# One-hots built as outer products of two small tables, and another order of VectorE's work at the end of the spread, in a two-layer encoder with product-key experts

## The chip, the cores and the metric

The kernel runs on one core of one Trainium2 chip. The metric is device time in microseconds (us), smaller is better. A core has TensorE (PE; its weight loads are shown apart, as PEld), VectorE (DVE), ScalarE (ACT), GpSimd (POOL) and SyncE (SP, which issues the DMAs here). Each works through its own queue in order, and waits on semaphores for the others.

## What is computed

Two layers over 256 tokens of width 1024: layer 0 is differential attention and an expert mixer (PEER), layer 1 is stick-breaking attention and another expert mixer. Each sub-layer is followed by a normalisation. Only the expert mixer matters for the change:

```
q = (x @ w_pq)                                  # 8 heads, two halves of 64
scores = q . sub_keys                           # 128 keys per half
s_top, i_top = top_k(scores, 16)                # per half
cand = s_top[0][:, None] + s_top[1][None, :]
g_s, g_i = top_k(cand, 16)                      # 16 of 256 candidates per head
id = i_top[0] * 128 + i_top[1]                  # one of 16384 experts
gate = softmax(g_s)
h = gelu(x . u[id]);   out = sum(gate * h * v[id])
```

A token chooses 8 heads x 16 = 128 experts. An expert's number is a row I (0 to 127) times 128 plus a column J (0 to 127).

## The kernel before

The kernel does the expert mixer without gathering. It computes gelu(x . u) for all 16384 experts as 128 units of 128 experts (a unit is one row I: all its columns J on the partitions, 256 tokens along the free axis), forms the matrix of gates in the same layout, multiplies both (the "weighing"), and multiplies by all of v. A product of two f32 numbers on TensorE is done in three passes, with each f32 operand split in a high part h (rounded by ScalarE, line 151) and a low part l = raw - h (VectorE or GpSimd, line 156). A unit of u or v is 512 KB: one DMA into `raw`, one h, one l. The rings of `raw`, `h` and `l` have 3 tiles each, so a DMA waits until the split of three units earlier has read its tile.

The stages of one expert mixer, in each of the two layers:

- **Routing** (`routing`, lines 669 to 781): scores, two top-16 searches, the arithmetic that turns the place among the candidates into I and J (`ef`), softmax of the gates (`gx`). Three transposes (lines 774 to 776) bring I, J and the gate to the layout "chosen expert on the partitions, token on the free axis", and ScalarE and VectorE put them into `idxT` as f16: row 0 is I, row 1 is J, rows 2 and 3 are the gate's high and low part. This is done once for each half b of the tokens. While it runs, TensorE computes the first 42 units of u ("stored" in `big`).
- **Spread** (lines 863 to 883): 32 iterations of 8 tokens. For a token, the 128x128 matrix of gates is the product of two one-hot matrices, summed over the 128 chosen experts: `oa` (I equals the column) and `gh`, `oj` (J equals the column, times the gate's high or low part). VectorE makes the four 1024-element f16 products of an iteration (lines 867, 868, 869, 872), TensorE does 16 small matmuls (878, 879) into two PSUM tiles, and `drain` of the next iteration takes them out: rows below 42 by VectorE, with the weighing (859), the others by ScalarE (860). Between the one-hot matmuls TensorE does 18 matmuls of the next units of u in each iteration (`next(ex)`, line 802); a unit has 24, so 3 iterations of 4 begin one, and with it `Hidden.pair` calls `fetch`, whose l is placed behind that iteration's one-hots in VectorE's order. The order of TensorE and VectorE is written out by hand here (`manual_schedule`). The five tiles of tag `oh` are shared by the three names.
- **Weighing and the product with v** (lines 911 to 957): for s = 0 to 64 the loop takes pair `order[s - 1]` of units, splits two units of v and does 24 passes (line 207). `prep(order[s])` makes wh and wl of the next pair's weighted activations (921, 922), and calls `weigh(2)`, which multiplies two more pairs by their gates (909). VectorE's order is by hand until s = 6, then the scheduler's.

At the end of the spread VectorE's order by hand is: last `drain`, `weigh(2)`, wl of pair 0, `weigh(2)`, l of unit 67 of u, l of unit 68, wl of pair 1, `weigh(2)`, l of the first two units of v, and so on. The l of unit 67 stands there since `pair` fetches a unit when it begins the one before.

Of the kernel before, what the change touches and what calls it, by code (L numbers as in the profile page):

```python
# [10 lines left out]
F32 = mybir.dt.float32  # L11
# [9 lines left out]
P = 128  # L21
# [6 lines left out]
HP = 8  # L28
# [30 lines left out]
def trunk(ctx: ExitStack, tc: tile.TileContext, x, xT, ln_g, ln_b, w_qkv, w_o_a, lam_p, subln, w_kv,  # L59
# [30 lines left out]
    nc.vector.tensor_scalar(ntri, jp, 0.0, -1.0, OP.is_le, OP.mult)  # L90
    nones = const.tile([P, P], F32, name="nones")
    nc.vector.memset(nones, -1.0)
    cmask = const.tile([P, P], BF16, name="cmask")
# [7 lines left out]
    nc.vector.tensor_copy(iota2, iota.unsqueeze(2).to_broadcast([P, P, 2]))  # L101
    off16 = const.tile([P, K, K], F16, name="off16")
    len16 = const.tile([P, K, K], F16, name="len16")
    for a, off, n in SPANS:
        nc.gpsimd.memset(off16[:, a, :], float(off))
        nc.gpsimd.memset(len16[:, a, :], float(SPANS[a - 1][2]) if a else 0.0)
    row16 = const.tile([P, K, K], F16, name="row16")
    nc.vector.tensor_copy(row16, iota[:, 0:K].unsqueeze(2).to_broadcast([P, K, K]))
    mhalf = const.tile([P, 8], F32, name="mhalf")
# [535 lines left out]
    def peer(layer, xh, xl, spill, o_res):  # L645
# [6 lines left out]
        for n in range(4):  # L652
            nc.scalar.activation(qp[:, 2 * n:2 * n + 2, :], aq[n], AF.Copy)
        idxT = work.tile([P, 4, T], F16, name="idxT", bufs=1)
        hx = {}

        def scores(b):
# [11 lines left out]
        def routing(b, sc):  # L669
# [16 lines left out]
            sm = reg(o + 1560, 2, HP)  # L686
            ef = reg(o + 1576, 2, HP, K)
            cc = half(o + 1832, HP, K)
            stp = half(o + 1896, HP, K, K)
            prd = half(o + 2920, HP, K, K)  # L690
            s16l = s16.rearrange("p h c k -> p (h c) k")
# [72 lines left out]
            yield 3.8  # L764
            ef = ef.rearrange("p c h k -> p (c h k)")
            gx = s16.rearrange("p h c k -> p (h c k)")[:, 0:P].rearrange("p (h k) -> p h k", k=K)
# [5 lines left out]
            yield 2.0  # L772
            pt = psum.tile([P, 3, P], F32, name="acc", tag="acc")
            nc.tensor.transpose(pt[:, 0, :], ef[:, 0:P], ident)
            nc.tensor.transpose(pt[:, 1, :], ef[:, P:2 * P], ident)
            nc.tensor.transpose(pt[:, 2, :], gx.rearrange("p h k -> p (h k)"), ident)
            bs = slice(b * P, (b + 1) * P)
            nc.scalar.activation(idxT[:, 0:2, bs], pt[:, 0:2, :], AF.Copy)
            nc.scalar.activation(idxT[:, 2, bs], pt[:, 2, :], AF.Copy, scale=GS)
            nc.vector.scalar_tensor_tensor(idxT[:, 3, bs], pt[:, 2, :], GS, idxT[:, 2, bs], OP.mult, OP.subtract)  # L780
            yield 0.5

        class Hidden:
# [77 lines left out]

        i2 = iota2.unsqueeze(1).to_broadcast([P, 4, P, 2])
        for t8 in range(0, T, 8):
            col = [idxT[:, c, t8:t8 + 8].rearrange("p (r t) -> p r t", t=2).unsqueeze(2).to_broadcast([P, 4, P, 2])
                   for c in range(4)]
            oj, gh, oa = (work.tile([P, 4, P, 2], F16, name=m, tag="oh", bufs=OH) for m in ("oj", "gh", "oa"))
# [48 lines left out]
        def prep(i):  # L915
# [7 lines left out]
            wq[i] = (wh, wl)  # L923
            weigh(2)

# [120 lines left out]
```

## Time and profile before

| | us |
|---|---|
| median of 3 runs | 1948.08 (1941.38 to 1950.44) |
| profiled execution, its own time | 1947.43 |
| its span, first to last instruction | 1945.7 |
| PE busy | 1861.1 (96%) |
| DVE busy | 1259.7 (65%) |
| ACT busy | 913.1 (47%) |
| POOL busy | 209.1 (11%) |

The span is what the trace covers; the profiled execution took 1.7 us more than that. A busy share is an average over stages: TensorE's 96% says where the work is, not what a single stage waits for.

### The profile page before, as it was taken

To read this page: it belongs to the slowest core of one execution; us is meant where nothing else is said; L and a number is where in the kernel's file an instruction comes from. 1 tells how busy PE (TensorE), PEld (TensorE's weight loads), DVE (VectorE), ACT (ScalarE), POOL (GpSimd) and SP (SyncE) were. 2 spreads that over 40 slices of the span, in tenths; PEclk is the share of its full clock that TensorE was granted. 3 is DMA by queue.
4 is the path that set the end of the run, shared out by engine and by line. 5 is a ranking of instruction groups with operands and counts; after the bars stand their busy time and mean duration, and the time that the engine had idled before them with its cause. 6 is when DMAs were issued, how large, how long until landed. Compare 5 with 4: busy or idle time off the path is not lost.

```text
span 1945.7 us, 30827 instructions
## 1 busy us (share of the span) xinstructions
PE 1861.1 (96%) x12244; PEld 1669.0 (86%) x12244; DVE 1259.7 (65%) x2300; ACT 913.1 (47%) x1244; POOL 209.1 (11%) x144
## 2 busy tenths in 40 slices
PE   8999999889999999999999899998899999999997
PEld 7779998887899999988798699988878999999886
DVE  5467988996455555565552479889865555555655
ACT  4444445444444444454446454454444444444543
POOL 5425400000000000000142253000000000000001
PEclk9888999999999999999999999999999999999999
DMA  6433544225555555565633235433355555555753
GB/s 218 170 119 119 179 147 152 99 98 179 189 192 189 193 179 190 191 240 192 211 128 133 109 131 184 151 132 109 107 186 176 194 183 186 195 183 184 249 194 131
DMA packets 90449, 325.40 MB, mean 167 GB/s; under 512 B 10176, under 2 KB 10560, under 8 KB 89664
## 3 DMA queue, kind: packets, MB, share of 16 engines
q1 hardware_dynamic: 90304, 323.43, 48.9%
q8 instruction: 96, 1.57, 0.3%
q14 instruction: 49, 0.40, 0.1%
HBM read 320.24 MB, written 3.15 MB: 166 GB/s over the span
## 4 chain that ended last, share of the span: by engine, by line
PE 77%; DVE 18%; issue 2%; DMA 1%; ACT 1%; POOL 0%; SPq 0%; ACTq 0%; DVEq 0%; POOLq 0%
PE acc L207 40%; PE w L802 26%; DVE l L156 3%; PE acc L252 2%; DVE gh L869 2%; DVE oj L872 2%; DVE oj L867 1%; PE acc L446 1%; DVE big L859 1%; PE w L252 1%; DVE big L330 1%; PE w L207 1%; PE w L468 1%; DVE big L699 1%; DVE big L701 1%
## 5 line engine op out<-in xcount | busy, mean ns | idle before, releaser
L151 ACT ACTIVATE h<-raw 128x1024 fp32r<-128x1024 f32 x579 | 607.0, 1058 | 850.4 <-PE acc L207 474.6
L156 DVE TENSOR_TENSOR l<-raw,h 128x1024 fp32r<-128x1024 f32 x526 | 642.9, 1234 | 537.4 <-ACT h L151 537.4
L802 PE MATMUL w<-xh,l 128*128 128x256 f32 x2048 | 580.4, 285 | 11.6 <-DVE l L156 10.9
L802 PE MATMUL w<-xh,h 128*128 128x256 f32 x2048 | 586.1, 286 | 1.8 <-ACT h L151 1.8
L802 PE MATMUL w<-xl,h 128*128 128x256 f32 x2048 | 580.4, 284 | 0.0
L802 PEld LDWEIGHTS w<-xh,l 128*128 128x128 f32 x2048 | 392.6, 192 | 18.5 <-DVE l L156 12.6
L207 PE MATMUL acc<-l,wh 128*128 128x512 f32 x1024 | 401.2, 393 | 7.4 <-DVE l L156 7.4
L207 PE MATMUL acc<-h,wl 128*128 128x512 f32 x1024 | 401.3, 393 | 0.0
L802 PEld LDWEIGHTS w<-xh,h 128*128 128x128 f32 x2048 | 393.9, 192 | 7.5 <-ACT h L151 2.3
L802 PEld LDWEIGHTS w<-xl,h 128*128 128x128 f32 x2048 | 393.7, 192 | 4.7
L207 PE MATMUL acc<-h,wh 128*128 128x512 f32 x1024 | 279.7, 392 | 1.6 <-ACT h L151 1.6
L207 PEld LDWEIGHTS acc<-l,wh 128*128 128x128 f32 x1024 | 193.7, 189 | 44.4 <-DVE l L156 7.8
L207 PEld LDWEIGHTS acc<-h,wl 128*128 128x128 f32 x1024 | 194.0, 189 | 37.2
L207 PEld LDWEIGHTS acc<-h,wh 128*128 128x128 f32 x1024 | 189.3, 189 | 38.0 <-ACT h L151 2.0
L156 POOL TENSOR_TENSOR l<-raw,h 128x1024 fp32r<-128x1024 f32 x53 | 127.8, 2415 | 174.3 <-ACT h L151 171.6
L180 POOL TENSOR_TENSOR ahead<-big,ahead 128x512 fp32r<-128x512 f32 x18 | 24.1, 1369 | 765.8 <-ACT ahead L170 765.8
L922 DVE TENSOR_TENSOR wl<-big,wh 128x512 fp32r<-128x512 f32 x128 | 86.9, 687 | 16.6 <-ACT wh L921 10.1
L879 PE MATMUL acc<-oa,oj 128*128 128x128 f16 x512 | 66.1, 220 | 28.8 <-DVE oj L872 28.8
L303 POOL TENSOR_TENSOR mv<-mv,mhalf 128x1 f32<-128x1 f32 x8 | 4.9, 607 | 762.9 <-DVE mv L302 762.9
L921 ACT ACTIVATE wh<-big 128x512 fp32r<-128x512 f32 x128 | 78.1, 619 | 13.0 <-DVE big L909 8.7
L879 PEld LDWEIGHTS <-oj 128*128 128x128 f16 x512 | 48.6, 97 | 35.1 <-DVE oj L872 35.0
L860 ACT ACTIVATE big<-acc 128x344 f32<-128x344 f32 x128 | 51.5, 453 | 49.3 <-DVE big L859 49.2
(210 smaller groups left out, 1855.7 us busy)
## 6 DMA issues: line engine op xcount, KB each, us to landing
raw<-in_uT SPq DMA_DIRECT2D x256, 512.0 KB, 3.4
raw<-in_v SPq DMA_DIRECT2D x256, 512.0 KB, 3.3
raw<-in_w_qkv SPq DMA_DIRECT2D x23, 512.0 KB, 4.0
raw<-in_w_kv SPq DMA_DIRECT2D x12, 512.0 KB, 4.0
raw<-in_w_o_a SPq DMA_DIRECT2D x8, 512.0 KB, 3.9
big<-in_w_pq SPq DMA_DIRECT2D x8, 512.0 KB, 6.7
raw<-in_w_pq SPq DMA_DIRECT2D x8, 512.0 KB, 5.6
raw<-in_w_q SPq DMA_DIRECT2D x8, 512.0 KB, 4.3
```

The lines of the kernel that those rows point to most:

```text
L151: self.h = nc.scalar.activation(h, raw, AF.Copy)
L156: o = e.tensor_tensor(l, raw, h.bitcast(F32), OP.subtract)
L180: o = nc.gpsimd.tensor_tensor(l[f], self.raws[d][:, f * 512:(f + 1) * 512], h[f].bitcast(F32), OP.subtract)
L207: nc.tensor.matmul(acc[b][f], a[:, d, ts], w[:, fs], start=(first and q == 0), stop=(last and q == 2))
L252: nc.tensor.matmul(acc[n // 2][:, n % 2, :], w[:, c:c + P], a[:, d, :], start=(d == 0 and q == 0 and n % 2 == 0), stop=(d == DC - 1 and q ...
L802: nc.tensor.matmul(ps[:, k, :], w[:, ds], a[:, d, :], start=(d == 0 and q == 0), stop=(d == DC - 1 and q == 2))
L860: nc.scalar.activation(wv[:, N_STORED:], pv[:, N_STORED:], AF.Copy, scale=1.0 / GS)
L869: nc.vector.tensor_tensor(gh, oj, col[2], OP.mult)
L872: nc.vector.tensor_tensor(oj, oj, col[3], OP.mult)
L879: nc.tensor.matmul(ps[:, k, :], oj[:, m, :, e], oa[:, m, :, e], start=False, stop=True)
L921: nc.scalar.activation(wh, s, AF.Copy)
L922: nc.vector.tensor_tensor(wl, s, wh.bitcast(F32), OP.subtract)
```

## The change

Each f16 column number J is written as 16 * (J >> 4) + (J & 15). A table of 8 columns says which J >> 4 a chosen expert has, one of 16 columns which J & 15, and a one-hot over 128 columns is the outer product of both. The gate is multiplied into the small table.

- Routing gains four VectorE instructions for each half of the tokens (a cast to integers, a shift, a mask, a cast back), a fourth transpose, and a fifth row of `idxT`.
- In the spread, `parts` runs once for 16 tokens (every second iteration) and makes `hi1` (which J >> 4, 128 elements), `lo` (256), `hi2` = hi1 times the gate's high part and `hi3` = hi1 times its low part (128 each). An iteration then has three large products in place of four: `oa`, `gh` = hi2 x lo, `oj` = hi3 x lo.
- `fetch` is called once more before the last `drain`, so that unit 67 is split ahead of it; `pair` then fetches only when fewer than two units are in hand.
- `weigh(2)` moves out of `prep`, and both stand behind the two splits of v in each step of the last loop.
- The tables `off16`, `len16` and `row16` of the routing move from a place of their own, filled once at the start, into `big`, filled by 48 memsets of GpSimd in each expert mixer. `nones` becomes a column read with step 0.

```diff
+        off16, len16, row16 = (
+            big[:, 17408 + i * 128:17408 + (i + 1) * 128].bitcast(F16).rearrange("p (a b) -> p a b", b=K) for i in range(3))
+        for a, off, n in SPANS:
+            nc.gpsimd.memset(off16[:, a, :], float(off))
+            nc.gpsimd.memset(len16[:, a, :], float(SPANS[a - 1][2]) if a else 0.0)
+            nc.gpsimd.memset(row16[:, a, :], float(a))
...
+            ei = i16.rearrange("p h c k -> p (h c k)").bitcast(I32).rearrange("p (c n) -> p c n", c=2)
+            nc.vector.tensor_copy(ei[:, 1], ef[:, 1])
+            nc.vector.tensor_scalar(ei[:, 0], ei[:, 1], 4, None, OP.logical_shift_right)
+            nc.vector.tensor_scalar(ei[:, 1], ei[:, 1], 15, None, OP.bitwise_and)
+            nc.vector.tensor_copy(ef[:, 1:3], ei)
...
-            pt = psum.tile([P, 3, P], F32, name="acc", tag="acc")
+            pt = psum.tile([P, 4, P], F32, name="acc", tag="acc")
...
             def pair(self, i, dst):
...
-                    self.fetch()
+                    if len(self.got) < 2:
+                        self.fetch()
...
+        NR = 8
+        hi1, hi2, hi3 = (work.tile([P, NR, 8, 2], F16, name=n, bufs=1) for n in ("hi1", "hi2", "hi3"))
+        lo = work.tile([P, NR, 16, 2], F16, name="lo", bufs=1)
+        def parts(t0):
...
+            nc.vector.tensor_tensor(hi1, i2[:, :, 0:8], col(1, 8), OP.is_equal)
+            nc.vector.tensor_tensor(lo, i2[:, :, 0:16], col(2, 16), OP.is_equal)
+            nc.vector.tensor_tensor(hi2, hi1, col(3, 8), OP.mult)
+            nc.vector.tensor_tensor(hi3, hi1, col(4, 8), OP.mult)
         for t8 in range(0, T, 8):
...
-            nc.vector.tensor_tensor(oj, i2, col[1], OP.is_equal)
-            nc.vector.tensor_tensor(oa, i2, col[0], OP.is_equal)
-            nc.vector.tensor_tensor(gh, oj, col[2], OP.mult)
+            if t8 % (2 * NR) == 0:
+                parts(t8)
+            rs = slice(t8 // 2 % NR, t8 // 2 % NR + 4)
+            def outer(dst, hi):
+                nc.vector.tensor_tensor(dst.rearrange("p r (a b) t -> p r a b t", b=16),
+                                        hi[:, rs].unsqueeze(3).to_broadcast([P, 4, 8, 16, 2]),
+                                        lo[:, rs].unsqueeze(2).to_broadcast([P, 4, 8, 16, 2]), OP.mult)
+            nc.vector.tensor_tensor(oa, i2, colI, OP.is_equal)
+            outer(gh, hi2)
             drain()
             prev = []
-            nc.vector.tensor_tensor(oj, oj, col[3], OP.mult)
+            outer(oj, hi3)
...
+        hidden.fetch()
         drain()
         ctx2.close()
...
         def prep(i):
...
             wq[i] = (wh, wl)
-            weigh(2)
...
-            if 0 < s < n:
-                prep(order[s])
-            if s == len(ext) // 2:
-                order_v.close()
             if s >= 1:
...
                             passes(acc, b, f, *args)
+                weigh(2)
+                if s < n:
+                    prep(order[s])
+            if s == len(ext) // 2:
+                order_v.close()
```

## Rows read from the trace of the kernel before

**Rows 1.** The page, busy us of each engine (share of the span) xinstructions.

```profile
PE 1861.1 (96%) x12244; PEld 1669.0 (86%) x12244; DVE 1259.7 (65%) x2300; ACT 913.1 (47%) x1244; POOL 209.1 (11%) x144
```

**Rows 2.** Windows by stage: us, busy us PE, PEld, DVE, ACT, POOL, PE clock, DMA.

```profile
314.00:426.00 112.00, 97.34 (x1015) 92.80 (x1014) 112.00 (x203) 51.99 (x94) 0.00 (x0) 1.00 0.32 109
...
504.00:830.00 326.00, 326.00 (x2089) 297.08 (x2088) 173.34 (x173) 148.24 (x174) 0.00 (x0) 1.00 0.56 188
```

**Rows 3.** Timeline of DVE in the spread of layer 0: start us, us, instruction.

```profile
334.51 0.68 DVE L872 TENSOR_TENSOR oj<-oj,idxT 128x1024 f16<-128x1024 f16 x1
335.11 1.22 DVE L156 TENSOR_TENSOR l<-raw,h 128x1024 fp32r<-128x1024 f32 x1
336.24 0.68 DVE L867 TENSOR_TENSOR oj<-iota,idxT 128x1024 f16<-128x1024 f16 x1
...
338.05 0.56 DVE L859 SCALAR_TENSOR_TENSOR big<-acc,big 128x168 f32<-128x168 f32 x2
338.53 0.68 DVE L872 TENSOR_TENSOR oj<-oj,idxT 128x1024 f16<-128x1024 f16 x1
```

**Rows 4.** Groups by form: shapes xcount | busy us, mean ns | idle before.

```profile
L867 DVE TENSOR_TENSOR oj<-iota,idxT 128x1024 f16<-128x1024 f16 x64 | 43.7, 682 | 4.1 <-ACT idxT L778 4.1
...
L752 DVE TENSOR_TENSOR big<-big,off 128x2048 f16<-128x2048 f16 x4 | 4.9, 1222 | 0.1
...
L740 DVE TENSOR_TENSOR big<-big 128x256 f16<-128x256 f16 x12 | 3.5, 292 | 0.4
...
L106 POOL MEMSET len<- 128x16 f16 x16 | 1.5, 115 | 0.0
```

**Rows 5.** Timeline of POOL before the first split of u, layer 0.

```profile
172.87 2.40 POOL L156 TENSOR_TENSOR l<-raw,h 128x1024 fp32r<-128x1024 f32 x1 [12.40 <-ACT h L151]
```

**Rows 6.** Timeline of DVE at the end of the routing, layer 0, second half.

```profile
300.99 0.28 DVE L769 TENSOR_REDUCE big<-big 128x8 f32<-128x128 f32 x1 [1.55 <-ACT big L768]
```

**Rows 7.** Timeline of DVE at the end of the spread, layer 0.

```profile
431.68 0.79 DVE L859 SCALAR_TENSOR_TENSOR big<-acc,big 128x168 f32<-128x168 f32 x2 [2.73 <-PE acc L879]
...
434.39 0.69 DVE L922 TENSOR_TENSOR wl<-big,wh 128x512 fp32r<-128x512 f32 x1
...
436.20 2.35 DVE L156 TENSOR_TENSOR l<-raw,h 128x1024 fp32r<-128x1024 f32 x2
444.08 0.69 DVE L922 TENSOR_TENSOR wl<-big,wh 128x512 fp32r<-128x512 f32 x1 [5.52 <-ACT wh L921]
...
445.89 2.35 DVE L156 TENSOR_TENSOR l<-raw,h 128x1024 fp32r<-128x1024 f32 x2
```

**Rows 8.** Timeline of ACT there: the split of v's second unit.

```profile
441.99 1.06 ACT L151 ACTIVATE h<-raw 128x1024 fp32r<-128x1024 f32 x1 [6.20 <-DMA raw<-in_v]
```

**Rows 9.** Timeline of PE there, with its waits; the last row is layer 1.

```profile
435.36 1.19 PE L207 MATMUL acc<-h,wh 128*128 128x512 f32 x4 [0.81 <-ACT h L151]
437.47 0.39 PE L802 MATMUL w<-xh,l 128*128 128x256 f32 x1 [0.93 <-DVE l L156]
...
447.16 0.80 PE L207 MATMUL acc<-l,wh 128*128 128x512 f32 x1 [4.15 <-DVE l L156]
...
1415.25 0.50 PE L207 MATMUL acc<-l,wh 128*128 128x512 f32 x1 [3.23 <-DVE l L156]
```

**Rows 10.** The chain that ended last: start us, us, what.

```profile
437.48 4.40 DMA raw<-in_v
447.16 56.66 PE acc L207 x236
...
521.13 2.75 PE acc L207 x12
...
1415.25 55.39 PE acc L207 x236
```

**Rows 11.** Window after that stall, columns as in rows 2.

```profile
446.00:450.00 4.00, 2.84 (x7) 2.29 (x8) 4.00 (x6) 0.55 (x2) 0.00 (x0) 0.55 0.43 139
```

More of the change, by code (lines that the diff above doesn't have):

```diff
@@ L90, in trunk @@
     nc.vector.tensor_scalar(ntri, jp, 0.0, -1.0, OP.is_le, OP.mult)
-    nones = const.tile([P, P], F32, name="nones")
-    nc.vector.memset(nones, -1.0)
+    none1 = const.tile([P, 1], F32, name="none1")
+    nc.vector.memset(none1, -1.0)
+    nones = none1.to_broadcast([P, P])
     cmask = const.tile([P, P], BF16, name="cmask")
@@ L653, in peer @@
             nc.scalar.activation(qp[:, 2 * n:2 * n + 2, :], aq[n], AF.Copy)
-        idxT = work.tile([P, 4, T], F16, name="idxT", bufs=1)
+        idxT = work.tile([P, 5, T], F16, name="idxT", bufs=1)
         hx = {}
+        off16, len16, row16 = (
[4 more added lines that the diff above has]
+            nc.gpsimd.memset(row16[:, a, :], float(a))
         def scores(b):
@@ L686, in routing @@
             sm = reg(o + 1560, 2, HP)
[L687 to L690, printed above, removed]
+            ef = reg(o + 1576, 3, HP, K)
+            cc = half(o + 1960, HP, K)
+            stp = half(o + 2024, HP, K, K)
+            prd = half(o + 3048, HP, K, K)
             s16l = s16.rearrange("p h c k -> p (h c) k")
@@ L772, in routing @@
             yield 2.0
-            pt = psum.tile([P, 3, P], F32, name="acc", tag="acc")
-            nc.tensor.transpose(pt[:, 0, :], ef[:, 0:P], ident)
-            nc.tensor.transpose(pt[:, 1, :], ef[:, P:2 * P], ident)
-            nc.tensor.transpose(pt[:, 2, :], gx.rearrange("p h k -> p (h k)"), ident)
+            pt = psum.tile([P, 4, P], F32, name="acc", tag="acc")
+            for c in range(3):
+                nc.tensor.transpose(pt[:, c, :], ef[:, c, :], ident)
+            nc.tensor.transpose(pt[:, 3, :], gx.rearrange("p h k -> p (h k)"), ident)
             bs = slice(b * P, (b + 1) * P)
-            nc.scalar.activation(idxT[:, 0:2, bs], pt[:, 0:2, :], AF.Copy)
-            nc.scalar.activation(idxT[:, 2, bs], pt[:, 2, :], AF.Copy, scale=GS)
-            nc.vector.scalar_tensor_tensor(idxT[:, 3, bs], pt[:, 2, :], GS, idxT[:, 2, bs], OP.mult, OP.subtract)
+            nc.scalar.activation(idxT[:, 0:3, bs], pt[:, 0:3, :], AF.Copy)
+            nc.scalar.activation(idxT[:, 3, bs], pt[:, 3, :], AF.Copy, scale=GS)
+            nc.vector.scalar_tensor_tensor(idxT[:, 4, bs], pt[:, 3, :], GS, idxT[:, 3, bs], OP.mult, OP.subtract)
             yield 0.5
@@ L862, in peer, with col @@
         i2 = iota2.unsqueeze(1).to_broadcast([P, 4, P, 2])
-        for t8 in range(0, T, 8):
-            col = [idxT[:, c, t8:t8 + 8].rearrange("p (r t) -> p r t", t=2).unsqueeze(2).to_broadcast([P, 4, P, 2])
-                   for c in range(4)]
-            oj, gh, oa = (work.tile([P, 4, P, 2], F16, name=m, tag="oh", bufs=OH) for m in ("oj", "gh", "oa"))
-            nc.vector.tensor_tensor(oj, i2, col[1], OP.is_equal)
-            nc.vector.tensor_tensor(oa, i2, col[0], OP.is_equal)
-            nc.vector.tensor_tensor(gh, oj, col[2], OP.mult)
+        NR = 8
+        hi1, hi2, hi3 = (work.tile([P, NR, 8, 2], F16, name=n, bufs=1) for n in ("hi1", "hi2", "hi3"))
+        lo = work.tile([P, NR, 16, 2], F16, name="lo", bufs=1)
+        def parts(t0):
+            def col(c, n):
+                a = idxT[:, c, t0:t0 + 2 * NR].rearrange("p (r t) -> p r t", t=2)
+                return a.unsqueeze(2).to_broadcast([P, NR, n, 2])
+            i2 = iota2.unsqueeze(1).to_broadcast([P, NR, P, 2])
+            nc.vector.tensor_tensor(hi1, i2[:, :, 0:8], col(1, 8), OP.is_equal)
+            nc.vector.tensor_tensor(lo, i2[:, :, 0:16], col(2, 16), OP.is_equal)
+            nc.vector.tensor_tensor(hi2, hi1, col(3, 8), OP.mult)
+            nc.vector.tensor_tensor(hi3, hi1, col(4, 8), OP.mult)
+        for t8 in range(0, T, 8):
+            if t8 % (2 * NR) == 0:
+                parts(t8)
+            rs = slice(t8 // 2 % NR, t8 // 2 % NR + 4)
+            colI = idxT[:, 0, t8:t8 + 8].rearrange("p (r t) -> p r t", t=2).unsqueeze(2).to_broadcast([P, 4, P, 2])
+            oj, gh, oa = (work.tile([P, 4, P, 2], F16, name=m, tag="oh", bufs=OH) for m in ("gl", "gh", "oa"))
+            def outer(dst, hi):
[4 more added lines that the diff above has]
+            outer(gh, hi2)
             drain()
             prev = []
-            nc.vector.tensor_tensor(oj, oj, col[3], OP.mult)
+            outer(oj, hi3)
             for r in range(2):
```

9 lines of the change are left out of this document (1 added, 8 removed).

## The prediction

> **What bounds the kernel now.** I read the page first. TensorE is busy for 96% of the span [rows 1], so for the kernel to get faster, TensorE has to wait less, or another engine has to stop holding it back; less work on VectorE, at 65%, is worth something only in a stage where TensorE waits for it. So I looked at windows by stage next. While u and v are both streamed (504 to 830 us) TensorE is busy for all of 326 us. In the spread of layer 0 it is busy for 97.34 of 112 us, and VectorE for all 112 [rows 2]: here VectorE is the limit. Layer 1 repeats this.
>
> The timeline of VectorE says what an iteration of the spread costs. A one-hot product lasts 0.68 us, but the next one starts 0.60 us after it: from 336.24, three of them bring us to the drain at 338.05. The two drains take 0.48, an l of u 1.13. From L872 at 334.51 to L872 at 338.53, one iteration with an l is 4.02 us [rows 3]; the iteration in four that begins no unit lacks the 1.13, so it is 2.89. Four iterations: 3 x 4.02 + 2.89 = 14.95 us, or 30 iterations in the 112 us window.
>
> Last, the end of the spread, where TensorE's timeline shows three waits in layer 0: 0.81, 0.93 and 4.15 us, together 5.89. In layer 1 the last of them is 3.23, the first two are the same: 4.97 [rows 9]. Here is how they come about. The last drain waits 2.73 us for the one-hot matmuls. Then VectorE does its list in order: wl of pair 0 at 434.39, and the l of units 67 and 68 only at 436.20 [rows 7]. TensorE waits for the first of these (the 0.93). The l of 67 also frees the raw tile for v's second unit: its DMA starts at 437.48 and takes 4.40 [rows 10], ScalarE waits 6.20 for it [rows 8], and wh of pair 1 is queued behind that split. VectorE waits 5.52 for this wh, and behind VectorE's wl stands the l of v's first unit, whose data were there long before; it comes at 445.89 [rows 7], and TensorE gets it at 447.16. One late split has put a DMA's latency on the path.
>
> The stall costs more than its idle time. After it the granted clock is 0.55 over four microseconds [rows 11], near the lower of the two levels (1.2 of 2.4 GHz), and the next 236 passes take 56.66 us in layer 0 and 55.39 in layer 1. At the later rate, 12 in 2.75 us, they are 54.08 [rows 10]: 2.6 and 1.3 us lost to the clock. So there is 5.89 + 2.6 = 8.5 us to be had in layer 0, and 4.97 + 1.3 = 6.3 in layer 1.
>
> **The change, part by part.**
>
> *The spread.* Each iteration loses one product of 1024 elements, 0.60 us; four iterations lose 2.41. `parts` is new, twice in four iterations: three instructions of 128 elements and one of 256, all f16. No row shows such small ones back to back, so I bound them. Two elements per cycle make 1024 elements 533 ns, and the 0.60 between starts leaves 0.07 for the instruction itself. By that, 128 elements are 0.136 and 256 are 0.20: 0.61 for one `parts`. From above: each lasts its full duration before the next starts. 256 elements f16 last 292 ns, 1024 last 682 [rows 4], so 128 last about 0.23, and the four 0.98, with gaps at most 1.1. I take 0.61: only hi2 depends closely on an earlier one, and `lo` stands between. Four iterations then are 14.95 - 2.41 + 2 x 0.61 = 13.76 us.
>
> Does the limit pass to TensorE? Its busy time of 97.34 us in 30 iterations [rows 2] is 13.0 for four, an upper bound since waiting at the start of a burst is counted in it. VectorE stays the limit, with less than a microsecond to spare; so a faster VectorE still would not bring much more. The saving is 1.19 us in four iterations, over 30 iterations of each layer: 7.5 x 1.19 x 2 = 17.9 us. With `parts` at 1.1 it is 7.5 x 0.21 x 2 = 3.2.
>
> This needs `gh` and `oj` to keep two elements per cycle although both operands are now repeated. The nearest rows: `col` of L867 repeats a pair of elements, as the small table does now, and L752 compares two operands that are both repeated; its 2048 elements take 1222 ns [rows 4], two per cycle too. So I take 0.60 for them. The third first-written tile of an iteration, which needs a tile that the last one-hot matmuls free, is now `oj`, behind the drain, and no longer `gh` ahead of it: no new wait.
>
> The Trainium skill speaks against small instructions here. "VectorE: DVE Perf Modes", section "The DRAIN you can't avoid", says that the next instruction does not start until the pipe has emptied, save one that is not held, and its section on the trn2 errata that many small tiles each pay a fixed cost. The trace shows starts 0.60 us apart at a duration of 0.68, so part of that is overlapped here; by the rule the saving would be that of the third rival.
>
> *The end of the spread.* l of unit 67 moves ahead of the last drain, into the 2.73 us in which VectorE waits there [rows 7]; at 1.13 us it costs nothing. If that wait were gone, it would cost its 1.13 per layer. The raw tile comes free about 7 us earlier, so v's second unit lands near 434.5 instead of 441.9. Behind wl of pair 0 (434.39, so done near 435.1) come the l of unit 68, then of v's first two units: 436.2, 437.3, 438.4. wl of pair 1 is now behind them and behind `weigh(2)`, near 440.3. TensorE has work until about 437 (the rest of iteration 31, unit 67) and may take unit 68 early, then needs v's first unit at 437, the second at 440, wl of pair 1 at 443. What is late next is the third unit of v, whose raw tile is freed by l of 68 at 436.2: 4.4 us of DMA, 1.06 of h and 1.2 of l make 442.9, just when it is wanted. I leave 1 us of waiting in each layer, and no loss of clock: 14.8 - 2.0 = 12.8 us gained. Bounds: 0 and 14.8.
>
> *The order in the loop over s.* wl of a pair now follows the two splits of v of its step. TensorE uses the second of these for 2.75 us before it wants that wl, and two weighings and a wl are less. Cost 0; that cover gone, the second rival shows the price of a wait.
>
> *Routing.* Four more instructions of 128 or 256 elements for each half, about 0.2 to 0.3 us each by the 292 ns row: 0.9 us, ahead of the softmax. There VectorE waits for ScalarE's exp, 1.55 us in the half that I show [rows 6], which hides them. Without it they would be 3.6 us in all. The fourth transpose and its longer eviction have no cover: some 0.4 us per layer, 0.8 in all.
>
> *Memsets.* 115 ns each at most, 48 per layer [rows 4]: under 5.5 us, while GpSimd idles for 12.40 us before its first split of u [rows 5]. Cost 0; if they were put in front of that split without cover, up to 11 us for both layers. `nones` read with step 0, and less work at the start: 0, as VectorE waits for x there.
>
> *Sum.* The profiled execution took 1947.4 us, span 1945.7 and 1.7 around it; it is 0.7 below the median, so no correction. 1947.4 - 17.9 - 12.8 + 0.8 = 1917.5 us.
>
> **The rivals.**
>
> 1. *The end of the spread keeps its stall in another form*: the faster start of v meets a DMA that is late, or wl of pair 1, now behind two splits, takes its place. For it: three raw tiles, and the third unit is due with no margin. Against it: v's second unit, the one that was late, gains 7 us. 1947.4 - 17.9 + 0.8 = 1930.3 us.
> 2. *The outer products run at one element per cycle* (the other side). Both operands are repeated, in different places. An f32 product of 1024 elements at that rate takes 1.13 us between starts [rows 3], 0.53 more for each of two products: four iterations gain 8 x 0.53 - 1.19 = 3.05 us, 7.5 x 3.05 x 2 = 45.8 us slower there: 1947.4 + 45.8 - 12.8 + 0.8 = 1981 us. It decides once each of the 128 products costs 0.23 us more (29.9 us in all). L752 speaks against it.
> 3. *Small instructions pay their whole duration*, and save little: `parts` at 1.0 to 1.1 us. For it: instructions that depend on one another, as hi2 on hi1. Against it: the starts of rows 3. 1947.4 - 3.2 - 12.8 + 0.8 = 1932 us.
> 4. *wl comes late in each step of the loop over s*: 0.61 us (a wl) in 64 steps of both layers would be 78 us, 1995 us. VectorE is busy for 173 of 326 us there [rows 2], which speaks against it.
>
> **How the numbers follow.** My forecast, 1917.5, has 0.62; the first rival 0.14, the third 0.11, the second 0.05, the fourth 0.03, and 0.05 is left for what I don't see, such as memsets or routing on the path. The range goes from 1909 (everything won, 1915, and a better clock at the start of the spread, too) to 1932, which takes in the first and third rival. About 0.5% (10 us) is what a measurement of this kernel tells from no change. Below 1938: the forecast, the first and the third rival, and some of the rest: 0.90. Within 0.5%: 0.04. Slower: 0.06.
>
> **What would show it.** Right: L867's place in an iteration gone, `gh` and `oj` still near 0.68 us, four small instructions within 0.65 us, an iteration pair shorter by 0.6; l of unit 67 ahead of the last drain; no wait of 4 us for a split of v, and the clock at 1.00 where rows 11 show 0.55. Wrong: `gh` near 1.2 us; a window of the spread in which TensorE is busy throughout (then it has become the limit); a wait for a DMA of v or for wl at the end of the spread; new waits of TensorE between 504 and 830.

## The result, and the profile after

| | before | after |
|---|---|---|
| median of the runs beside each other, us | 1947.61 (6 runs, 1941.29 to 1950.44) | 1922.97 (6 runs, 1921.08 to 1926.48) |
| ratio, 95% interval | | 0.9881 (0.9865 to 0.9897) |
| profiled execution, its span, us | 1947.43, 1945.7 | 1923.61, 1921.8 |

The kernel became 24.6 us faster by the medians; the ratio, taken over all runs, says 1.2%. The forecast was 1917.5: the time is in the range, and 5.5 us above the forecast. The spread gave what was forecast, its end gave more, and its start lost what was not forecast. The table shows it part by part. The line numbers of after are its own: L879 to L882 are `parts`, L896 is `oa`, L892 `gh` and `oj` (its tile is now called gl), L145 and L150 are h and l, L783 the eviction into `idxT`, L811 the gelu, L808 and L201 the passes over u and v, L865 the drain, L951 wl.

| part, us, layer 0 / layer 1 | before | after | change, both layers | forecast |
|---|---|---|---|---|
| start: from the row of 336 passes over u to the first large product of the second iteration | 88.60 / 88.62 | 93.84 / 92.63 | +9.25 | +0.8 |
| spread: from there to the last drain | 118.44 / 118.78 | 109.39 / 110.15 | -17.68 | -17.9 |
| end: from there to the first stretch of 30 passes over u | 72.14 / 69.95 | 62.75 / 62.74 | -16.60 | -12.8 |
| all else of the span | | | +1.1 | 0 |

The borders are starts of rows: in layer 0 before, 224.64 (336 passes), 313.24 (L867), 431.68 [rows 7] and 503.82 (30 passes); after, 224.87, 318.71 (L896), 428.10 and 490.85. The sum of the first three parts is called the stage below: 279.18 and 277.35 us before, 265.98 and 265.52 after. Each stage is read from one execution, and two layers of one kernel differ by up to 1.8 us, so differences well under 1 us say little.

The page's busy line (answers to rows 1), then windows in the spread, behind its end and in the streaming of u and v (columns as in rows 2):

```profile
PE 1853.7 (96%) x12248; PEld 1665.9 (87%) x12248; DVE 1241.8 (65%) x2379; ACT 914.5 (48%) x1244; POOL 212.6 (11%) x208
```

```profile
330.00:386.00 56.00, 52.68 (x554) 50.89 (x553) 56.00 (x128) 28.20 (x51) 0.00 (x0) 1.00 0.34 114
...
446.00:450.00 4.00, 4.00 (x19) 3.31 (x18) 4.00 (x6) 1.81 (x3) 0.00 (x0) 1.00 0.58 207
...
502.00:818.00 316.00, 316.00 (x2027) 287.99 (x2026) 168.75 (x169) 145.02 (x170) 0.00 (x0) 1.00 0.56 189
```

The busy shares of the page have hardly moved; the windows say more. In the spread VectorE is still busy throughout and TensorE for 94% (87% in rows 2). At 446 the clock is 1.00, not the 0.55 of rows 11. While u and v are streamed TensorE does not wait at all, so the new place of wl in that loop costs nothing.

VectorE's timeline in the spread of layer 0 (answers to rows 3):

```profile
335.89 0.22 DVE L879 TENSOR_TENSOR hi<-iota,idxT 128x128 f16<-128x128 f16 x1
336.02 0.29 DVE L880 TENSOR_TENSOR lo<-iota,idxT 128x256 f16<-128x256 f16 x1
336.23 0.23 DVE L881 TENSOR_TENSOR hi<-hi,idxT 128x128 f16<-128x128 f16 x1
336.36 0.23 DVE L882 TENSOR_TENSOR hi<-hi,idxT 128x128 f16<-128x128 f16 x1
336.50 0.69 DVE L896 TENSOR_TENSOR oa<-iota,idxT 128x1024 f16<-128x1024 f16 x1
337.10 0.69 DVE L892 TENSOR_TENSOR gh<-hi,lo 128x1024 f16<-128x1024 f16 x1
...
338.18 0.69 DVE L892 TENSOR_TENSOR gl<-hi,lo 128x1024 f16<-128x1024 f16 x1
...
418.48 0.24 DVE L879 TENSOR_TENSOR hi<-iota,idxT 128x128 f16<-128x128 f16 x1
```

`parts` takes 0.61 us from its first start to the start of `oa`. The outer products take 0.69 us, 0.60 between starts, as the products that they replace. From 335.89 to 418.48 lie six times four iterations: 13.77 us each.

VectorE at the end of the spread of layer 0 (answers to rows 7), then the chain (to rows 10):

```profile
425.11 1.23 DVE L150 TENSOR_TENSOR l<-raw,h 128x1024 fp32r<-128x1024 f32 x1 [0.22 <-ACT h L145]
428.10 0.79 DVE L865 SCALAR_TENSOR_TENSOR big<-acc,big 128x168 f32<-128x168 f32 x2 [1.76 <-PE acc L907]
...
430.82 0.69 DVE L951 TENSOR_TENSOR wl<-big,wh 128x512 fp32r<-128x512 f32 x1
431.43 2.36 DVE L150 TENSOR_TENSOR l<-raw,h 128x1024 fp32r<-128x1024 f32 x2
434.50 1.23 DVE L150 TENSOR_TENSOR l<-raw,h 128x1024 fp32r<-128x1024 f32 x1 [0.72 <-ACT h L145]
...
437.04 0.69 DVE L951 TENSOR_TENSOR wl<-big,wh 128x512 fp32r<-128x512 f32 x1
439.82 1.23 DVE L150 TENSOR_TENSOR l<-raw,h 128x1024 fp32r<-128x1024 f32 x1 [2.09 <-ACT h L145]
```

```profile
224.87 40.58 PE w L808 x336
...
441.86 48.99 PE acc L201 x216
490.85 3.59 PE w L808 x30
```

Unit 67 is split at 425.11, in the wait ahead of the last drain. Nothing on VectorE waits longer than 2.09 us here, and TensorE's timeline from 426 to 452 has no wait at all, where rows 9 have three. The passes over v that follow run at 0.227 us each (48.99 / 216); rows 10 have 0.240.

Now the start of the spread, where the loss is. ScalarE of the kernel before, then of the kernel after, at the end of the first half's routing in layer 0:

```profile
277.80 0.38 ACT L778 ACTIVATE idxT<-acc 128x256 f16<-128x256 f32 x1 [1.52 <-PE acc L776]
...
278.23 1.06 ACT L151 ACTIVATE h<-raw 128x1024 fp32r<-128x1024 f32 x1
279.31 1.28 ACT L805 ACT_TABLE_LOAD   x1
```

```profile
278.53 1.06 ACT L145 ACTIVATE h<-raw 128x1024 fp32r<-128x1024 f32 x1 [2.03 <-PE w L808]
279.61 1.28 ACT L811 ACT_TABLE_LOAD   x1
280.91 0.60 ACT L811 ACTIVATE big<-w 128x512 f32<-128x512 f32 x1
281.40 0.48 ACT L783 ACTIVATE idxT<-acc 128x384 f16<-128x384 f32 x1
```

Before, ScalarE waits for the transposes and evicts them (copies them from PSUM into `idxT`) at once; the split, the table load and the gelu come behind. After, the last transpose is done near 278.7 (it starts at 278.40 and takes 0.27 us), but the eviction stands behind a split, a table load and a gelu in ScalarE's queue, and begins at 281.40. What that does, first VectorE and TensorE before, then after, then TensorE's windows after:

```profile
278.21 0.69 DVE L867 TENSOR_TENSOR oj<-iota,idxT 128x1024 f16<-128x1024 f16 x1 [2.02 <-ACT idxT L778]
...
283.23 2.35 DVE L156 TENSOR_TENSOR l<-raw,h 128x1024 fp32r<-128x1024 f32 x2
```

```profile
284.50 0.39 PE L802 MATMUL w<-xh,l 128*128 128x256 f32 x1 [3.15 <-DVE l L156]
```

```profile
281.92 0.23 DVE L879 TENSOR_TENSOR hi<-iota,idxT 128x128 f16<-128x128 f16 x1 [5.51 <-ACT idxT L783]
...
286.94 2.35 DVE L150 TENSOR_TENSOR l<-raw,h 128x1024 fp32r<-128x1024 f32 x2
```

```profile
288.22 0.58 PE L808 MATMUL w<-xh,l 128*128 128x256 f32 x1 [6.43 <-DVE l L150]
```

```profile
282.00:288.00 6.00, 0.00 (x0) 0.00 (x0) 6.00 (x12) 1.00 (x2) 0.00 (x0) 0.87 0.00 0
288.00:294.00 6.00, 5.78 (x30) 5.79 (x31) 5.73 (x12) 0.84 (x1) 0.00 (x0) 0.56 0.50 175
```

VectorE waits 5.51 us for `idxT`; before, 2.02. Behind that product in its order stand two splits of u, and TensorE waits 6.43 us for them, not 3.15. After the idle stretch the granted clock is 0.56 over six microseconds, near 1.2 of 2.4 GHz. Layer 1 repeats both waits: 5.50 and 6.43.

GpSimd's 48 memsets in each layer don't show. Its first split of u comes where it came in rows 5:

```profile
172.84 2.40 POOL L150 TENSOR_TENSOR l<-raw,h 128x1024 fp32r<-128x1024 f32 x1 [12.29 <-ACT h L145]
```

### The profile page after: what moved, and what is told of

The parts are those of the page before. It is cut to its first block, busy times and chain, and to the rows that moved or that the text cites. A ratio compares the mean times of both kernels' runs of the same rounds, so it can differ in the third digit from the quotient of the medians.

```text
span 1921.8 us, 30897 instructions
## 1 busy us (share of the span) xinstructions
PE 1853.7 (96%) x12248; PEld 1665.9 (87%) x12248; DVE 1241.8 (65%) x2379; ACT 914.5 (48%) x1244; POOL 212.6 (11%) x208
## 3 DMA queue, kind: packets, MB, share of 16 engines
HBM read 320.24 MB, written 3.15 MB: 168 GB/s over the span
## 4 chain that ended last, share of the span: by engine, by line
PE 80%; DVE 16%; issue 2%; DMA 1%; ACT 1%; POOL 0%; SPq 0%; ACTq 0%; POOLq 0%
PE acc L201 40%; PE w L808 28%; PE acc L246 4%; DVE l L150 3%; DVE gl L892 2%; DVE big L865 2%; DVE gh L892 2%; PE acc L440 1%; DVE oa L896 1%; PE w L246 1%; DVE big L324 1%; PE w L201 1%; PE w L462 1%; DVE big L699 1%; DVE big L701 1%
## 5 line engine op out<-in xcount | busy, mean ns | idle before, releaser
L145 ACT ACTIVATE h<-raw 128x1024 fp32r<-128x1024 f32 x579 | 607.5, 1060 | 853.2 <-PE acc L201 474.5
L150 DVE TENSOR_TENSOR l<-raw,h 128x1024 fp32r<-128x1024 f32 x526 | 645.0, 1238 | 533.8 <-ACT h L145 533.6
L808 PE MATMUL w<-xh,l 128*128 128x256 f32 x2048 | 579.6, 284 | 16.5 <-DVE l L150 16.5
L808 PE MATMUL w<-xh,h 128*128 128x256 f32 x2048 | 585.7, 286 | 2.1 <-ACT h L145 2.1
L808 PE MATMUL w<-xl,h 128*128 128x256 f32 x2048 | 580.0, 283 | 0.0
L808 PEld LDWEIGHTS w<-xh,l 128*128 128x128 f32 x2048 | 392.5, 192 | 22.4 <-DVE l L150 17.4
L808 PEld LDWEIGHTS w<-xh,h 128*128 128x128 f32 x2048 | 393.5, 192 | 7.9 <-ACT h L145 2.5
L201 PE MATMUL acc<-h,wl 128*128 128x512 f32 x1024 | 399.1, 391 | 0.0
L201 PE MATMUL acc<-l,wh 128*128 128x512 f32 x1024 | 398.7, 390 | 0.0
L808 PEld LDWEIGHTS w<-xl,h 128*128 128x128 f32 x2048 | 393.4, 192 | 4.8
L201 PE MATMUL acc<-h,wh 128*128 128x512 f32 x1024 | 278.1, 390 | 0.0
L201 PEld LDWEIGHTS acc<-h,wl 128*128 128x128 f32 x1024 | 192.8, 188 | 36.9
L201 PEld LDWEIGHTS acc<-l,wh 128*128 128x128 f32 x1024 | 192.5, 188 | 36.4
L201 PEld LDWEIGHTS acc<-h,wh 128*128 128x128 f32 x1024 | 188.1, 188 | 35.6
L150 POOL TENSOR_TENSOR l<-raw,h 128x1024 fp32r<-128x1024 f32 x53 | 128.2, 2421 | 169.7 <-ACT h L145 156.2
L951 DVE TENSOR_TENSOR wl<-big,wh 128x512 fp32r<-128x512 f32 x128 | 87.0, 687 | 6.3 <-PE acc L201 5.7
L907 PE MATMUL acc<-oa,gl 128*128 128x128 f16 x512 | 66.3, 220 | 14.5 <-DVE gl L892 13.0
L906 PE MATMUL acc<-oa,gh 128*128 128x128 f16 x512 | 70.4, 220 | 0.2 <-DVE gh L892 0.2
```

Source lines behind the costliest of these rows:

```text
L145: self.h = nc.scalar.activation(h, raw, AF.Copy)
L150: o = e.tensor_tensor(l, raw, h.bitcast(F32), OP.subtract)
L201: nc.tensor.matmul(acc[b][f], a[:, d, ts], w[:, fs], start=(first and q == 0), stop=(last and q == 2))
L906: nc.tensor.matmul(ps[:, k, :], gh[:, m, :, e], oa[:, m, :, e], start=True, stop=False)
L907: nc.tensor.matmul(ps[:, k, :], oj[:, m, :, e], oa[:, m, :, e], start=False, stop=True)
L951: nc.vector.tensor_tensor(wl, s, wh.bitcast(F32), OP.subtract)
```

## The experiments

All times are compared with runs of the kernel before beside them, whose medians were 1948.97 us for e1 to e4 and between 1947.4 and 1947.8 for the others; the ratio compares with those runs. The stage is measured as above, in the profiled execution: from the start of the row of 336 passes to that of the first 30 passes; e3, e10 and e11 reached it 6 to 7 us later than the kernel before in that execution, which the stage leaves out.

| run | from, and what differs | median, us | ratio, 95% interval | stage, layer 0 / 1 |
|---|---|---|---|---|
| before | | 1947.61 | 1 | 279.18 / 277.35 |
| after | | 1922.97 | 0.9881 (0.9865 to 0.9897) | 265.98 / 265.52 |
| e1 | before, new end alone | 1930.67 | 0.9912 (0.9884 to 0.9941) | 269.86 / 269.06 |
| e2 | after, old end | 1943.52 | 0.9966 (0.9947 to 0.9985) | 276.14 / 275.91 |
| e7 | before, early fetch alone | 1934.34 | 0.9935 (0.9913 to 0.9957) | 271.09 / 272.10 |
| e8 | before, new order alone | 1932.37 | 0.9917 (0.9896 to 0.9938) | 270.97 / 270.89 |
| e6 | after, `parts` twice | 1946.83 | 0.9997 (0.9981 to 1.0013) | 276.62 / 276.30 |
| e3 | after, eviction ahead | 1918.25 | 0.9839 (0.9816 to 0.9863) | 264.07 / 262.99 |
| e4 | after, split ahead | 1914.42 | 0.9821 (0.9797 to 0.9846) | 261.32 / 261.33 |
| e9 | after, eviction ahead, first product late | 1914.56 | 0.9822 (0.9786 to 0.9858) | 260.82 / 262.26 |
| e5 | before, new routing alone | 1957.0 | 1.0049 (1.0032 to 1.0066) | 284.23 / 283.51 |
| e10 | e5, split ahead | 1952.47 | 1.0022 (1.0005 to 1.0039) | 280.04 / 279.55 |
| e12 | e10, eviction ahead | 1943.9 | 0.9985 (0.9973 to 0.9996) | 277.14 / 276.67 |
| e11 | before, split ahead | 1943.63 | 0.9974 (0.9958 to 0.9990) | 276.63 / 276.26 |

**The two halves of the change: e1 and e2.** e1 is the kernel before with the early fetch and the new order of weighing and wl:

```diff
-                    self.fetch()
+                    if len(self.got) < 2:
+                        self.fetch()
...
+        hidden.fetch()
         drain()
...
-            weigh(2)
...
-            if 0 < s < n:
-                prep(order[s])
...
+                weigh(2)
+                if s < n:
+                    prep(order[s])
```

> The kernel before with only the other order at the end of the spread (fetch ahead of the last drain, weighing and prep behind the splits of v); routing and one-hots as before. If the late split of unit 67 alone made the stall, this gives nearly all that the stage gained in the changed kernel, some 16 us: 1931 us (1929 to 1934), and no wait of 4 us for a split of v. Rival: the stall shrank because VectorE comes to the end with time in hand in a shorter spread; then less than half of it, 1939 us or more.

e2 is the kernel after with those lines as they were before.

> The changed kernel with the order at the end of the spread as before; outer products, routing and tables as changed. If the parts add up, the spread gives 17 to 18 us and the routing takes back 9 to 10: 1939 us (1937 to 1942), with the 4 us wait for a split of v at the end of the spread still there. Rival: the shorter spread also removes that stall; then about 1925 to 1931 us.

Against the runs beside them the end alone gives 18.3 us and the rest alone 5.4; by the stages 17.6 and 4.5 of the 25.0 that both give together. e1 came as expected, e2 1.5 us slower than its range. So the new one-hots, worth 17.7 us in the spread, come with a loss that is in their half, which the table by parts puts at their start. The parts don't quite add up, and e2 says why: with the old end a faster spread only comes sooner to the late unit of v. TensorE waits for v's splits there for 9.5 us in two waits, 7.4 in the kernel before [rows 9, the two of 4.15 and 3.23].

**Is VectorE still the limit of the spread: e6.** The second run of `parts` writes the same values again.

```diff
             if t8 % (2 * NR) == 0:
                 parts(t8)
+                parts(t8)
```

> The kernel after, with parts run twice in each second iteration (the second time it writes the same values): 16 more runs of 0.61 us in each layer. Theory (VectorE still sets the pace of the spread): the time grows by all of it, 19.5 us less what falls where VectorE waits, so 1938 to 1943, and TensorE's waits for the one-hots grow. Rival (TensorE has become the limit of the spread, with under 1 us to spare in four iterations): less than half, under 1933.

Nearly all of it reaches the time, and more than expected: 23.9 us by the medians, 21.4 by the stages. The timeline of VectorE shows why a repeat costs more than 0.61. The last of the first run and the first of the second:

```profile
336.55 0.22 DVE L882 TENSOR_TENSOR hi<-hi,idxT 128x128 f16<-128x128 f16 x1
336.80 0.23 DVE L879 TENSOR_TENSOR hi<-iota,idxT 128x128 f16<-128x128 f16 x1
```

`hi1` is written anew while the instruction ahead still reads it, so here the next start comes 0.25 us later and not 0.14. A repeat takes 0.72 us (336.08 to 336.80), 32 of them 23.0. VectorE sets the pace; the rival, TensorE as the limit, which expected less than half, falls.

**Which half of the new end does it: e7 and e8.** e7 is the first two hunks of e1's diff, e8 the other three.

> The kernel before with the early fetch alone: unit 67 of u is split ahead of the last drain; weighing and wl stay where they were. Theory (one late split put a DMA on the path; either half of the change takes it away, so they are substitutes): v's second unit lands about 7 us earlier, VectorE's wait for wh of pair 1 of 5.5 us is gone, at least two thirds of the 17 us are gained: 1931 to 1936. Rival (both halves are needed, wl of pair 1 still stands ahead of v's first split): less than half, 1940 to 1947.

> The kernel before with the other order alone: weighing and wl of the next pair behind the two splits of v; unit 67 is split where it was, so v's second unit still lands late, near 442. Theory (substitutes): v's first unit no longer waits behind wl of pair 1 and is split near 438.5, TensorE has work until about 443, and waits 1 to 2 us for v's second unit; two thirds of the 17 us or more are gained, 1931 to 1937. Rival (both needed): the late unit costs as much as before, less than half is gained, 1940 to 1947.

Each of them alone brings most of it, by the stages 13.3 and 14.7 us of the 17.6 that both bring, so they largely replace each other, though neither brings all. Each breaks the chain of rows 7 to 9 at another link. In e7, VectorE's timeline and TensorE's one wait there:

```profile
437.85 0.69 DVE L924 TENSOR_TENSOR wl<-big,wh 128x512 fp32r<-128x512 f32 x1 [1.54 <-ACT wh L923]
...
439.66 2.36 DVE L156 TENSOR_TENSOR l<-raw,h 128x1024 fp32r<-128x1024 f32 x2
```

```profile
440.94 0.50 PE L207 MATMUL acc<-l,wh 128*128 128x512 f32 x1 [1.31 <-DVE l L156]
```

ScalarE has no wait for a DMA there, wl waits 1.54 and not 5.52 us, and of TensorE's 4.15 us 1.31 are left. In e8 the unit is as late as it was; VectorE, then ScalarE:

```profile
435.01 3.49 DVE L156 TENSOR_TENSOR l<-raw,h 128x1024 fp32r<-128x1024 f32 x3
442.21 1.23 DVE L156 TENSOR_TENSOR l<-raw,h 128x1024 fp32r<-128x1024 f32 x1 [3.72 <-ACT h L151]
```

```profile
441.12 1.06 ACT L151 ACTIVATE h<-raw 128x1024 fp32r<-128x1024 f32 x1 [5.32 <-DMA raw<-in_v]
```

ScalarE still waits 5.32 us for the DMA, but v's first unit is split right behind unit 68, in the row x3 at 435.01, and TensorE works on it meanwhile: it is busy for all of 440 to 444.

**The start, in the kernel after: e3, e4, e9.** e3 moves ScalarE's eviction of the first half's routing ahead of the table load and the gelu that stood in front of it, and of the split that follows; in the second half the eviction stays behind a table load and a gelu. Its core:

```diff
+            self.seen += 1
+            if self.first and self.seen == 2:
+                queue_after(self.h, self.first)
...
-            nc.scalar.activation(idxT[:, 3, bs], pt[:, 3, :], AF.Copy, scale=GS)
+            units.first = nc.scalar.activation(idxT[:, 3, bs], pt[:, 3, :], AF.Copy, scale=GS)
+            units.seen = 0
...
-                nc.scalar.activation(dst, ps.rearrange("p a b -> p (a b)"), AF.Gelu)
+                g = nc.scalar.activation(dst, ps.rearrange("p a b -> p (a b)"), AF.Gelu)
+                if units.first:
+                    queue_after(g, units.first)
+                    units.first = None
```

> The changed kernel, and in ScalarE's queue the eviction of idxT is put ahead of the table load and the gelu that stand in front of it (the split h stays ahead). If the stall at the start of the spread comes from ScalarE's order, the first small one-hot starts 1.5 to 2 us earlier in each layer, TensorE's wait of 6.4 us shrinks to about 4.7, and the kernel takes 3 to 5 us less than the changed one: 1918 to 1920 us. Rival: the four added instructions of VectorE make it late; then the wait stays at 6.4 us and the time at 1923.

e4 leaves ScalarE as it is and changes VectorE's order: the splits of u stand ahead of the wait for `idxT`, and the first small product behind the routing of the second half.

```diff
+            if b == 0:
+                yield 2.3
-            nc.vector.scalar_tensor_tensor(idxT[:, 4, bs], pt[:, 3, :], GS, idxT[:, 3, bs], OP.mult, OP.subtract)
+            units.routed = nc.vector.scalar_tensor_tensor(idxT[:, 4, bs], pt[:, 3, :], GS, idxT[:, 3, bs], OP.mult, OP.subtract)
...
-            nc.vector.tensor_tensor(hi1, i2[:, :, 0:8], col(1, 8), OP.is_equal)
+            o = nc.vector.tensor_tensor(hi1, i2[:, :, 0:8], col(1, 8), OP.is_equal)
+            if t0 == 0:
+                queue_after(o, units.routed)
```

> The changed kernel, with one more split of u ahead of VectorE's wait for idxT in the first half of the routing, and the first iteration's one-hots behind the whole routing. If TensorE's 6.4 us wait is only that split standing in the queue behind VectorE's wait, it falls to 2 us or less in each layer and the clock does not drop: 8 to 12 us less than the changed kernel, 1911 to 1915 us. Rival: VectorE's total work sets the start of the spread; then the wait only moves, and the gain is under 3 us.

e9 is e3 with e4's last three lines and the name `units.routed`, without the `yield`.

> The kernel after with ScalarE's eviction into idxT ahead of the table load and the gelu, and VectorE's first small product queued behind the routing's last idxT instruction; the split of u isn't held back by hand. Theory (there is one stall at the start of the spread, and each of the two edits tried so far takes it away at another place): no better than the better of the two, 1913 to 1917. Rival (the two gains, 4.7 and 8.6 us, stand for different stalls and add up): 1910 or less.

e3 takes 1.9 and 2.5 us from the stage: VectorE's wait falls to 3.58 us, TensorE's to 4.52. e4 takes 4.7 and 4.2, with VectorE's wait for `idxT` still 4.32 us long in layer 0. It no longer holds up TensorE, since two splits now stand ahead of it:

```profile
276.11 2.57 DVE L150 TENSOR_TENSOR l<-raw,h 128x1024 fp32r<-128x1024 f32 x2
```

The windows of e4 that answer to those of after:

```profile
282.00:288.00 6.00, 4.71 (x37) 4.30 (x37) 4.93 (x6) 3.46 (x6) 0.00 (x0) 1.00 0.02 9
288.00:294.00 6.00, 6.00 (x53) 6.00 (x52) 5.73 (x12) 2.22 (x3) 0.00 (x0) 1.00 0.74 257
```

TensorE works 10.71 of these 12 us, 5.78 in the kernel after, at clock 1.00.

e9 came as its theory said and is no better than e4. That does not show that there is only one stall, because e9 is not both edits in full: without the `yield` only one split stands ahead of VectorE's wait, and TensorE waits for the next:

```profile
287.26 0.39 PE L814 MATMUL w<-xh,l 128*128 128x256 f32 x1 [2.52 <-DVE l L155]
```

The changed kernel with both edits in full was not run; the kernel before with the new routing and both edits is e12 below, and there the second edit adds to the first. e4 is the fastest kernel here by its median, with e9 0.1 us behind: 34.6 us below the runs of the kernel before beside it, and 8.9 below the changed kernel by the stages.

**The start, in the kernel before: e5, e10, e12, e11.** Is it the routing that brings the stall, or `parts` at the start of the spread? e5 is the kernel before with the routing of the change (and `nones` as a column), the old one-hots and the old end.

```diff
+            nc.vector.tensor_copy(ei[:, 1], ef[:, P:2 * P])
+            nc.vector.tensor_scalar(ei[:, 0], ei[:, 1], 4, None, OP.logical_shift_right)
+            nc.vector.tensor_scalar(ei[:, 1], ei[:, 1], 15, None, OP.bitwise_and)
+            nc.vector.tensor_copy(ej.rearrange("p (c n) -> p c n", c=2), ei)
...
+            nc.tensor.transpose(pt[:, 2, :], ej[:, 0:P], ident)
...
-            nc.scalar.activation(idxT[:, 0:2, bs], pt[:, 0:2, :], AF.Copy)
+            nc.scalar.activation(idxT[:, 0:3, bs], pt[:, 0:3, :], AF.Copy)
```

> The kernel before with the routing of the change alone: four more VectorE instructions, a fourth transpose, the longer first eviction; the one-hots are made as before, the end of the spread stays as before. Theory (the start of the spread lost what the prediction did not see, because ScalarE's eviction into idxT came behind one more split, the table load and the gelu): about 9 us slower than the kernel before, 1956 (1953 to 1959), 4 to 5.5 us of it in each layer between the first passes over u and the first products of the second iteration; VectorE's first product waits about 5.5 us for that eviction, TensorE about 6 us for the split of u behind it. Rival (the routing costs what I predicted, 0.8 us, and the 9.5 us come from the new one-hots at the start of the spread, parts above all): 1948.5.

9.4 us slower, with the two waits of the kernel after. The list of waits from 260 to 300 us (us in all, times, longest):

```profile
PE w L810 <- DVE l L157: 6.4, 1, 6.4
DVE oj L875 <- ACT idxT L786: 5.4, 1, 5.4
```

So the routing does it alone; no new one-hot is needed for it. The next question is whether its instructions cost that, or their place in the queues. e10 is e5 with e4's edit (its product is `oj`, at L867 in the kernel before).

> The kernel before with the routing of the change, as in the run before, and the split of u ahead of the first product that reads idxT. Theory (what the routing cost is the place of that split in VectorE's queue, not its instructions): nearly all of the 9.4 us come back, 1945 to 1950. Rival (the fourth transpose, the longer eviction and the four instructions have a price of their own of 2 us or more in each layer): 1952 to 1957.

This missed. Only 4.5 us came back by the medians (4.2 and 4.0 by the stages), and the time lies where the rival put it. But part of this is a gain that the old routing could have had as well, so the comparison that counts is e11, the kernel before with the same edit and the old routing:

> The kernel before with nothing but the split of u ahead of the first product that reads idxT. Theory (the kernel before has the same stall in a smaller form: VectorE waits 2.02 us for idxT there, TensorE 3.15 us for the split): 2 to 3.5 us in each layer, 1941 to 1944. Rival (only the change made it a stall; before, the wait had cover): 1946 to 1949.

e11's time is in the expected range; the stage gains 2.55 us in layer 0 and only 1.09 in layer 1, less than expected there. So the kernel before had the stall in a small form, and about 3.6 of the 8.9 us that e4 gains could have been had without the change. e10's stage is 3.41 and 3.29 us longer than e11's. In e10 ScalarE has the order of the kernel after:

```profile
285.03 1.28 ACT L815 ACT_TABLE_LOAD   x1
286.32 0.60 ACT L815 ACTIVATE big<-w 128x512 f32<-128x512 f32 x1
286.81 0.48 ACT L786 ACTIVATE idxT<-acc 128x384 f16<-128x384 f32 x1
```

and VectorE's whole routing of the second half stands behind the instruction that waits for this eviction. VectorE's wait there is 4.21 us. e12 is e10 with e3's edit.

> The kernel of the run before last (the kernel before, with the change's routing, and the split of u ahead of the first product that reads idxT), and beside that ScalarE's eviction into idxT ahead of the table load and the gelu; the orders of VectorE and of the instructions of the routing stay. In that run the stage was 3.4 and 3.3 us longer than with the old routing, and the first half's idxT came 3.4 us later. Theory (this too is ScalarE's order, now by way of the second half's routing, which stands behind idxT on VectorE): the table load and the gelu, 1.9 us, no longer stand ahead of the eviction, so the stage gets 1.5 to 2 us shorter in each layer and the time falls from 1952.5 to 1947.5 to 1950. Rival (it is the price of the added instructions themselves): 1951.5 to 1953.5.

The time fell by 8.6 us, the stage by 2.90 and 2.88; both are more than expected, and the 2.8 us between them are not traced. VectorE's wait for `idxT` falls from 4.21 to 2.30 us. ScalarE in e12:

```profile
277.73 0.47 ACT L791 ACTIVATE idxT<-acc 128x384 f16<-128x384 f32 x1
...
278.38 1.28 ACT L821 ACT_TABLE_LOAD   x1
```

What is left between e12 and e11 is 0.51 and 0.41 us by the stages, and 0.3 by the medians. The orders are the same but for one split of ScalarE, which e12 has ahead of the first half's eviction and e11 behind it. So the price of the routing's instructions is of the size of 1 us in all, too small to be told from the noise. Nearly all the rest of e5's loss is the order of two queues.

## Why the prediction was nearly right

- *The spread: right.* `parts` takes the 0.61 us taken for it, four iterations 13.77 for 13.76, and 17.7 us came for 17.9. VectorE stayed the limit (e6). The second rival is out by 0.60 us between starts of `gh` and `gl`. The third is out by 0.13 to 0.21 us between the starts of the small products, which last 0.22 to 0.29. The Trainium skill, "VectorE: DVE Perf Modes", section "The DRAIN you can't avoid", lets the next instruction start only when the pipe is empty, unless it is not held; the rows show the exception, for small products too.
- *The end: mechanism right, size low.* The forecast put wl of pair 1 near 440.3 and the end of the third unit's l near 442.9 on the old times; the last drain came 3.58 us earlier, so 436.7 and 439.3. The wl came at 437.04, the l ended at 441.05 (439.82 and 1.23), 1.7 late, and not by the DMA on which the forecast built it: ScalarE's split ahead of it, at 438.73, waits 1.73 us for TensorE. Even so TensorE has no wait there, so the 1 us per layer kept for it was not needed. The gain was 16.6 us, above the upper bound of 14.8. The bound took 0.229 us a pass (12 in 2.75) for the passes behind the stall, which take 0.227: 236 of them make 0.55 us per layer, 1.1 in all. The other 0.7 is not traced to a row. The first rival, a stall in another form, did not come. What the prediction told as one chain has two links, and breaking either alone brings three quarters or more of the gain (e7, e8).
- *The start and the routing: here is the error.* The term was 0.8 us, "the fourth transpose and its longer eviction have no cover: some 0.4 us per layer". As a price of those instructions it fits: e12 against e11 gives 0.51 and 0.41, though that is within the noise. So does the cover of the four VectorE instructions: the wait for exp behind them fell from 2.60 to 1.62 us in the first half of layer 0. It holds while a table load delays exp anyway; in e12, in the second half, exp itself waits 2.45 us for VectorE (0.24 in e11). But the term priced instructions where they stood, and they did not stay. ScalarE's order is not written by hand here; in the built program the eviction came behind a split, a table load and a gelu, and VectorE's order had splits of u behind the product that waits for it. The term came to 9.25 us.
- *Memsets, `nones`, the order in the loop over s: right, 0.* Rows at 172.84 and of the window from 502 show it. The fourth rival did not come.
- *The sum:* against its own profiled execution the forecast was 6.1 us low: the start by 8.45, all else of the span by 1.1, the spread by 0.2, less the end's 3.8, which make 6.0. That it came this near is partly luck: the end's surplus, which was not forecast, hid almost half of the error at the start.

It is shown that the order of ScalarE's and VectorE's queues makes the loss: the new routing alone brings it into the kernel before (e5), and with both orders put right there all but some 0.9 us of it is gone (e12 against e11). In the changed kernel e3 and e4 each take a part of it away; how much both in full would take is open. Why the program's builder placed the eviction there is not shown; nor is the 1.1 us outside the three parts, of which 0.95 lies between the stage of layer 0 and that of layer 1.

## What to carry to other kernels

Where a change lengthens a chain across engines, price the new instructions, and then look at the queue of each engine they pass through: a consumer that comes a little later may be put behind a table load, and its wait holds up everything behind it on the next engine. A wait costs what stands behind it. In the changed kernel moving one split ahead of the wait gave 8.9 us by the stages, and shortening the wait 4.4; in the kernel before, shortening it gave another 5.8 after the split had been moved, since the routing of the second half still stood behind it. When a stall has several links in series, try each cure alone, since one may do most of it, and then both in full.

## What was not expected of the hardware

- The gap between the starts of two small VectorE instructions depends on whether the second has to do with the one just ahead. With 128 elements, at a duration of 0.22 or 0.23 us, it is 0.13 to 0.14 where it has not, and 0.25 where it overwrites what the one ahead reads (e6). The routing's shift, mask and cast back, each of which reads or overwrites what the one ahead has used, start 0.26 us apart; here are shift and mask in layer 0, second half, of the kernel after:

```profile
303.12 0.23 DVE L768 TENSOR_SCALAR big<-big 128x128 int32<-128x128 int32 x1
303.38 0.23 DVE L769 TENSOR_SCALAR big<-big 128x128 int32<-128x128 int32 x1
```

So the third rival had a point: by these rows hi2 directly behind hi1 would have started some 0.25 us after it (an estimate, no run has it); with `lo` between, no start is later than 0.21.

- One wait of 6.43 us of TensorE cost more than itself: over the six microseconds behind it the granted clock was 0.56, and 30 matmuls were done in them. In e4, where TensorE's waits in the same place are 0.79 and 0.50 us, the clock stayed at 1.00, with 53 matmuls in the same window.
